# A four-layer diffusion backbone: gate products of a GLA head moved between its own levels, low-rank gates in two passes, and products moved ahead of the first attention scores

## The chip, the cores and the metric

The kernel runs on one NeuronCore of a Trainium2 chip. TensorE (PE) multiplies matrices, VectorE (DVE), ScalarE (ACT) and GpSimd (POOL) do elementwise work, and SyncE (SP) and ACT issue most of the DMAs. The metric is the device time of one execution in microseconds; a kernel's time is the median of its runs.

## The reference

A latent stream of 512 tokens and a context stream of 256 tokens, each 1024 wide, run through four layers. Layer i uses mixer i % 3: layers 0 and 3 are a bidirectional chunked GLA (gated linear attention, 4 heads), layer 1 is a windowed attention with a sink, layer 2 a bidirectional RG-LRU. Layer 3 gives no context output (`ctx_out` is false there).

```python
def mixer_gla(h_lat, h_ctx, w_in, w_g1, w_g2, b_g, g_head, w_out, ctx_out):
    def project(h):
        q, k, v, z = jnp.split(h @ w_in, [GLA_DK, 2 * GLA_DK, 2 * GLA_DK + GLA_DV], axis=-1)
        la_f, la_b = [split_heads(jax.nn.log_sigmoid(((h @ w_g1[d]) @ w_g2[d] + b_g[d]).astype(jnp.float32)) / GLA_TAU, GLA_HEADS)
                      for d in range(2)]
        ...
    def finish(o, z):
        o = merge_heads(rmsnorm(o, g_head[:, None, :]))
        return (o.astype(z.dtype) * jax.nn.silu(z)) @ w_out
...
    for i in range(DEPTH):
        ...
        h = rmsnorm(x, g_pre[i]) * (1.0 + scale[:, None, :]) + shift[:, None, :]
        ...
        x = x + gate[:, None, :] * rmsnorm(y, g_post[i])
```

Here `w_g1` is the low-rank gate (rank 16, two directions), and z is the gate product: each head's output is multiplied by silu(z) before the product with `w_out`.

## The kernel before

All activations lie transposed in SBUF: a tile holds 128 features on its partitions and the 768 tokens along its free axis (512 latent, "lat", then 256 context, "ctx"). A product with full precision is made of three matmul passes: every operand is split into a rounded part and a remainder (`Rh`, `Rl` for activations, `wh`, `wl` for weights), and Rh·wh, Rl·wh and Rh·wl are summed in PSUM. A 128-column block of weights over both streams is 8 contraction steps × 3 passes × two widths: 24 matmuls of 256 columns and 24 of 512.

**Stages.** `first_norm` (0 to 62 us) normalises the input, makes the modulation of layer 0 (L524) and begins the first products (L728), among them the g1 product. Then come GLA layer 0 (62 to 370 us), `finish` of layer 0 (products with w_out, L796), attention, its finish, RG-LRU, its finish, GLA layer 3 (about 1207 to 1460 us) and its finish.

**Weights.** `plan(i)` yields a layer's weight blocks in the order in which they are multiplied. `loadw` issues the DMAs of a block (two pieces of 512 KB, on SP's queue), and `convert` splits it: an ACT copy to `wh` (L266) and a DVE subtraction to `wl` (L269). `weights(key)` hands out the next block, and keeps up to two ahead. `load_g1` (L271 on) loads the 32 columns of the low-rank gate, and splits them four times over into four 32-column groups of a `wh` and a `wl` tile (L287), so that the product `t` = g1·h comes out four times on 128 partitions. The gate product (L979) uses 96 of these, against a three-group tile `g2`.

**A GLA head.** For each head h: `gates(h)` makes its decays, `project(h)` its q and k (L385), and `levels` walks over the levels of a chunk from the smallest up (L1062 score matmuls of 24 pieces, with X, Y and K made by DVE, ACT and POOL before them). Between the levels, `spread` deals out matmuls of a side stream: a generator that yields each matmul with its cost in columns. The side stream is z(h-1), then v(h) (L1034): the gate product of the head before and the head's own values. Head 0 has no head before, and so v(0) alone. `outputs(h)` comes in the next head: transposes (L1155), state updates (L1166), output products (L1194), the head's norm, and transposes back (L1207). The gate product z of a head (`z_steps`, its matmuls at L395) ends in silu, and is multiplied with the head's output in `OG`: whichever of the two comes first writes `OG`, and the other multiplies (`put` keeps account). Head 3's outputs come after the loop, and then z(3): `run(outputs(*prev))`, `run(zgates(GH - 1))`. A scheduler then sets the final order by priorities, and may pull those z products up between the output's steps.

**Attention.** `fill(n)` puts n columns' worth of waiting product matmuls (L395) into the program; the loop over the heads' blocks calls it after the scores of each block (L1458 to L1475), then transposes the probabilities (L1516) and multiplies them with v (L1532).

## Time and profile before

| | us |
|---|---|
| median of 3 runs | 1517.19 (1516.3 to 1522.14) |
| the profiled execution | 1513.64 |
| its span in the trace | 1511.8 |
| PE busy | 1442.0 (95%) |
| DVE busy | 1010.5 (67%) |
| ACT busy | 784.2 (52%) |
| GLA layer 0, 62 to 370.05 | 308.1 |
| GLA layer 3, 1207 to 1460.82 | 253.8 |

The trace is that of one execution, whose own time is 1513.64 us, 3.55 us under the median; 1.8 us of it lie outside the span. A matmul's row gives its whole duration; one starts before the last one's end, so what a stream of matmuls costs is the distance between starts. A value in square brackets behind a row is the idle time ahead of it, with what ended it. "Clock" is TensorE's granted clock as a share of 2.4 GHz.

### The profile page before, as it was taken

What the parts mean: (1) busy time and instruction counts of PE and PEld (TensorE: products, weight loads), DVE (VectorE), ACT (ScalarE), POOL (GpSimd) and SP (SyncE); (2) the same over time, 40 slices, a digit from 0 to 9 for tenths busy, and PEclk for the clock granted to TensorE, in tenths of its full rate; (3) what the DMA queues carried; (4) which work ended last, traced back from release to release, by engine and by line L of the source; (5) the groups of instructions that cost most, each with busy time, mean ns of one, the idle gap of its engine ahead of it and who ended that gap; (6) DMA issues with size and microseconds to landing.
All of it is one profiled execution on the core that took longest, in us unless ns stands there. A gap on an engine that the chain in (4) does not pass through costs nothing.

```text
span 1511.8 us, 29077 instructions
## 1 busy us (share of the span) xinstructions
PE 1442.0 (95%) x11691; PEld 1206.4 (80%) x11691; DVE 1010.5 (67%) x1914; ACT 784.2 (52%) x1541; POOL 189.4 (13%) x300
## 2 busy tenths in 40 slices
PE   5988999999999899999999999899999999999998
PEld 3877888888877778878888787788878778889886
DVE  5576657576264389787883568988972667676854
ACT  5535353624252367656662477878842555364441
POOL 2202100112022200010000210000011211101111
PEclk8999999999999999999999999999999999999999
DMA  9441514112574542122216625212252342121232
GB/s 300 145 147 53 169 38 135 57 34 76 203 237 140 174 112 68 31 65 57 57 56 224 217 79 152 82 50 71 67 177 64 103 145 91 46 60 57 60 111 85
DMA packets 153046, 162.35 MB, mean 107 GB/s; under 512 B 12418, under 2 KB 141968, under 8 KB 152912
## 3 DMA queue, kind: packets, MB, share of 16 engines
q1 hardware_dynamic: 147456, 146.56, 31.4%
q10 hardware_dynamic: 5456, 13.94, 2.6%
q8 instruction: 92, 1.51, 0.4%
q14 instruction: 42, 0.34, 0.1%
HBM read 138.44 MB, written 11.53 MB: 99 GB/s over the span
## 4 chain that ended last, share of the span: by engine, by line
PE 54%; DVE 10%; ACT 5%; DMA 4%; issue 2%; SPq 1%; POOL 1%; ACTq 0%; DVEq 0%; POOLq 0%
PE mxt L796 14%; PE pjt L395 9%; PE pjt L385 9%; PE pjt L1034 4%; PE mxt L1532 3%; PE mxt L1516 2%; PE sct L1637 2%; PE mxt L524 1%; PE mxt L1475 1%; PE mxt L1194 1%; DVE wl L269 1%; PE mxt L1458 1%; DMA bb<-in_b_mod_dram 1%; DMA raw<-in_w_mod_dram 1%; PE sct L1062 1%
## 5 line engine op out<-in xcount | busy, mean ns | idle before, releaser
L385 PE MATMUL pjt<-Rh,wh 128*128 128x256 f32 (+1 forms) x592 | 199.0, 337 | 5.3 <-DVE Rh L649 3.3
L385 PE MATMUL pjt<-Rl,wh 128*128 128x256 f32 (+1 forms) x592 | 198.2, 336 | 2.0 <-DVE Rl L650 1.6
L385 PE MATMUL pjt<-Rh,wl 128*128 128x256 f32 (+1 forms) x592 | 197.1, 334 | 0.7 <-DVE wl L269 0.7
L269 DVE TENSOR_TENSOR wl<-raw,wh 128x1024 fp32r<-128x1024 f32 x106 | 129.7, 1237 | 51.2 <-ACT wh L266 50.6
L395 PE MATMUL pjt<-Rh,wl 128*128 128x512 f32 (+1 forms) x448 | 160.3, 358 | 0.0
L395 PE MATMUL pjt<-Rl,wh 128*128 128x512 f32 (+1 forms) x448 | 159.8, 357 | 0.0
L395 PE MATMUL pjt<-Rh,wh 128*128 128x512 f32 (+1 forms) x448 | 159.5, 356 | 0.0
L266 ACT CAST wh<-raw 128x1024 fp32r<-128x1024 f32 x118 | 121.4, 1051 | 71.6 <-PE mxt L796 33.0
L796 PE MATMUL mxt<-wh,Rh 128*128 128x512 f32 x352 | 138.9, 395 | 0.0
L796 PE MATMUL mxt<-wh,Rl 128*128 128x512 f32 x352 | 137.6, 391 | 0.8 <-DVE Rl L769 0.8
L796 PE MATMUL mxt<-wl,Rh 128*128 128x512 f32 x352 | 137.2, 390 | 0.0
L385 PEld LDWEIGHTS pjt<-Rh,wh 128*128 128x128 f32 x592 | 112.5, 191 | 17.0 <-DVE Rh L649 4.4
L385 PEld LDWEIGHTS pjt<-Rl,wh 128*128 128x128 f32 x592 | 112.6, 190 | 14.6 <-DVE Rl L650 3.8
L385 PEld LDWEIGHTS pjt<-Rh,wl 128*128 128x128 f32 x592 | 112.6, 191 | 12.6 <-DVE wl L269 1.2
L1034 PE MATMUL pjt<-wl,Rh 128*128 128x256 f32 x384 | 110.6, 288 | 0.0
L1034 PE MATMUL pjt<-wh,Rh 128*128 128x256 f32 x384 | 109.8, 286 | 0.0
L1034 PE MATMUL pjt<-wh,Rl 128*128 128x256 f32 x384 | 109.5, 285 | 0.0
L1494 ACT ACTIVATE pe<-mxt,mxs 128x256 f32<-128x256 f32 (+2 forms) x128 | 70.7, 556 | 52.6 <-DVE mxs L1486 51.9
L395 PEld LDWEIGHTS pjt<-Rh,wl 128*128 128x128 f32 x448 | 84.6, 189 | 9.8 <-issue 1.9
L395 PEld LDWEIGHTS pjt<-Rh,wh 128*128 128x128 f32 x448 | 84.7, 189 | 9.2 <-issue 1.2
L395 PEld LDWEIGHTS pjt<-Rl,wh 128*128 128x128 f32 x448 | 84.7, 189 | 9.2 <-issue 1.3
L804 DVE TENSOR_TENSOR y<-mxt,gpt 128x512 f32<-128x512 f32 x44 | 30.3, 689 | 73.9 <-ACT y L803 73.8
(295 smaller groups left out, 3480.9 us busy)
## 6 DMA issues: line engine op xcount, KB each, us to landing
rawp<-in_w_mod_dram SPq DMA_DIRECT2D x48, 512.0 KB, 5.8
raw<-in_w_mod_dram SPq DMA_DIRECT2D x48, 512.0 KB, 4.4
raw<-in_a_w_in_dram SPq DMA_DIRECT2D x32, 512.0 KB, 3.5
raw<-in_b_w_in_dram SPq DMA_DIRECT2D x20, 512.0 KB, 4.9
raw<-in_c_w_in_dram SPq DMA_DIRECT2D x20, 512.0 KB, 3.6
xd<-x SPq DMA_DIRECT2D x18, 512.0 KB
raw<-in_a_w_out_dram SPq DMA_DIRECT2D x16, 512.0 KB, 3.5
x<-xd ACTq DMA_DIRECT2D x16, 512.0 KB, 8.9
```

The source lines that it names most:

```text
L266: S.copy(h, x)
L269: e.tensor_tensor(l, x, h.bitcast(F32), op=ALU.subtract)
L385: PE.matmul(ps, w[u][:, k, c0 : c0 + P], R[v][:, k, t0 : t0 + n], start=(k == 0 and u + v == 0), stop=(k == KC - 1 and u == 1),)
L395: PE.matmul(ps, w[u][:, k, c0 : c0 + P], R[x][:, k, t0 : t0 + n], start=(k == 0 and u + x == 0), stop=(k == KC - 1 and u == 1),)
L524: PE.matmul(ps[32 * g : 32 * g + 32, 0:256], sT[:, k, :], r2[k // 4][:, k % 4, :], start=(n < 4), stop=(n >= 4), skip_group_check=True,)
L796: PE.matmul(ps, l[:, tt * P : (tt + 1) * P], r, start=(k == 0 and u + v == 0), stop=(k == kc - 1 and u == 1),)
L804: V.tensor_tensor(y[tt][:, c], ps, gpt[:, 1 if tt >= 4 else 0, c], op=ALU.mult)
L1034: PE.matmul(ps[:, n, :], R[u][:, k, tt * P : (tt + 1) * P], w[x][:, k, :], start=(k == 0 and u + x == 0), stop=(k == KC - 1 and u == 1),)
L1494: S.activation(p[:, o : o + w], u[e][:, :w], AF.Exp, bias=nm, scale=0.125, accum_out=den[:, n : n + 1],)
L1516: PE.transpose(u[e][:, c * P : (c + 1) * P], ps[e][:, m * P : (m + 1) * P], ident)
L1532: PE.matmul(po[64 * e : 64 * e + 64, 0:P], v[:, keys[m], 64 * kv : 64 * kv + 64], pt[:, e, m * P : (m + 1) * P], start=(m == len(keys) - 1 ...
L1637: PE.matmul(ps[:, t0 : t0 + nn], wg[a][:, n, :], x[c][:, p0 : p0 + nn], start=(q == 0), stop=(q == 2),)
```

## The change

Three things are changed.

- **g1 in two passes.** `load_g1` makes one tile with four 32-column groups: the rounded weights three times and their remainder once (one ACT copy from the raw tile, one DVE subtraction, two more ACT copies). `terms(w)` then gives two passes, w·Rh and w·Rl, in place of three: the low-order weight product comes out on partitions of its own. `g2` gets a fourth row group (one more DMA of 32 KB on each of the ACT and SP queues), and the gate matmul contracts over 128 partitions instead of 96.
- **z with its own head.** In `plan` and in the loop over heads, heads 0 to 2 have z(h) and then v(h) as side stream. In head 3 the side stream is v(3), then the first half of z(3) (e = 0); the second half (e = 1) comes after the outputs.
- **Attention.** `fill(2300)` is called once more, ahead of the first block's scores.

```diff
--- before.py
+++ after.py
@@ -270,6 +270,7 @@
 
     def load_g1(a):
 
         r = raw()
         rv = r.rearrange("p a b -> p (a b)")[:, 0:256].rearrange("p (k r) -> p k r", k=KC)
         for d in range(2):
@@ -279,13 +280,12 @@
             )
 
         def convert():
-            w1h = wp.tile([P, KC, 256], F32R, name="wh", tag="wh")
-            w1l = wp.tile([P, KC, 256], F32R, name="wl", tag="wl")
-            for g in range(4):
-                c = slice(32 * g, 32 * g + 32)
-                S.copy(w1h[:, :, c], rv)
-                V.tensor_tensor(w1l[:, :, c], rv, w1h[:, :, c].bitcast(F32), op=ALU.subtract)
-            return w1h, w1l
+            w1 = wp.tile([P, KC, 256], F32R, name="wh", tag="wh")
+            S.copy(w1[:, :, 0:32], rv)
+            V.tensor_tensor(w1[:, :, 96:128], rv, w1[:, :, 0:32].bitcast(F32), op=ALU.subtract)
+            for g in range(1, 3):
+                S.copy(w1[:, :, 32 * g : 32 * g + 32], w1[:, :, 0:32].bitcast(F32))
+            return (w1,)
 
         return convert
 
@@ -299,7 +299,7 @@
         if load:
             g2_loaded.append(a)
             for d in range(2):
-                for g in range(3):
+                for g in range(4):
                     (nc.sync if d else nc.scalar).dma_start(
                         r[32 * g + 16 * d : 32 * g + 16 * d + 16, d, :], I["a_w_g2"][a, d]
                     )
@@ -324,10 +324,9 @@
             qk = lambda h: (f"qk{h}", cols(w, (h * P, P), (512 + h * P, P)))
             v = lambda h: (f"v{h}", cols(w, (1024 + h * GDV, GDV)))
             z = lambda h: (f"z{h}", cols(w, (2048 + h * GDV, GDV)))
-            yield from (qk(0), v(0))
-            for h in range(1, GH):
-                yield from (qk(h), z(h - 1), v(h))
-            yield z(GH - 1)
+            for h in range(GH - 1):
+                yield from (qk(h), z(h), v(h))
+            yield from (qk(GH - 1), v(GH - 1), z(GH - 1))
         elif kind == 1:
             w, wo = I["b_w_in"][0], I["b_w_out"][0]
             q = lambda g: (f"q{g}", cols(w, (g * 256, 256)))
@@ -377,14 +376,18 @@
 
     begun = {}
 
+    def terms(w):
+        return ((0, 0), (0, 1), (1, 0)) if len(w) > 1 else ((0, 0), (0, 1))
     def ws_part(w, c0, ps, t0, n):
 
         R = (Rh, Rl)
         for k in range(KC):
-            for u, v in ((0, 0), (0, 1), (1, 0)):
+            for u, v in terms(w):
                 PE.matmul(
                     ps, w[u][:, k, c0 : c0 + P], R[v][:, k, t0 : t0 + n],
-                    start=(k == 0 and u + v == 0), stop=(k == KC - 1 and u == 1),
+                    start=(k == 0 and u + v == 0), stop=(k == KC - 1 and (u, v) == terms(w)[-1]),
                 )
 
     def product_steps(ps, w, c0, t0, n):
@@ -724,11 +727,11 @@
             for w, c0, stream, ps in sel:
                 t0, n = STREAM[stream]
                 for k in ks:
-                    for u, v in ((0, 0), (0, 1), (1, 0)):
+                    for u, v in terms(w):
                         PE.matmul(
                             ps, w[u][:, k, c0 : c0 + P], (Rh, Rl)[v][:, k, t0 : t0 + n],
                             start=(k == 0 and u + v == 0 and not (w is wqk and stream == "ctx")),
-                            stop=(k == KC - 1 and u == 1), skip_group_check=True,
+                            stop=(k == KC - 1 and (u, v) == terms(w)[-1]), skip_group_check=True,
                         )
 
         with tc.manual_schedule(engines={PE.engine, S.engine, V.engine}):
@@ -943,6 +946,7 @@
             keep_pool.append(1)
             g2r = load_g2(a)
             w1 = weights("g1")
             t1 = mp.tile([P, T], F32R, name="t1")
             for stream in ("ctx", "lat"):
                 t0, n = STREAM[stream]
@@ -953,7 +957,7 @@
                 )
 
             g2 = mp.tile([P, 2, 512], F32R, name="g2")
-            S.copy(g2[:96], g2r[:96])
+            S.copy(g2, g2r)
             G.tensor_tensor(g2[32:64], g2r[32:64], g2[32:64].bitcast(F32), op=ALU.subtract)
 
             gated = {}
@@ -977,7 +981,7 @@
                     for stream in ("ctx", "lat"):
                         t0, n = STREAM[stream]
                         PE.matmul(
-                            ps[:, t0 : t0 + n], g2[:96, d, h * P : (h + 1) * P], t1[:96, t0 : t0 + n],
+                            ps[:, t0 : t0 + n], g2[:, d, h * P : (h + 1) * P], t1[:, t0 : t0 + n],
                             start=True, stop=True,
                         )
                     S.activation(tmp[:, pl, :], ps[:, :T], AF.Abs, bias=b)
@@ -1250,9 +1254,13 @@
                     background(1)
                     yield
 
-            def zgates(h):
-                w = weights(f"z{h}")
-                for e in range(2):
+            wz = {}
+            def zgates(h, es=(0, 1)):
+                if h not in wz:
+                    wz[h] = weights(f"z{h}")
+                w = wz[h]
+                for e in es:
                     for stream in ("ctx", "lat") if ctx_out else ("lat",):
                         yield from z_steps(mp, w, e, 2 * h + e, put, (stream,))
 
@@ -1275,7 +1283,6 @@
                 Y = mp.tile([P, 2, T], F32, name="Y", tag="Y", bufs=2)
                 pr = project(h, q, Y)
                 os = outputs(*prev) if prev else iter(())
-                z = zgates(h - 1) if prev else iter(())
                 next(pr)
                 next(os, None)
                 next(pr)
@@ -1302,15 +1309,19 @@
                     vl.rearrange("p d t -> p (d t)").rearrange("p (c n) -> p c n", c=6),
                 )
 
-                side = chain(z, values(h, v))
                 nz = len(STREAM) * T if ctx_out else len(STREAM) * TL
-                nz = nz if prev else 0
-                spread(lv, side, len(LEVELS), 24 * (nz + 4 * GDV) / 2.4)
+                if h < GH - 1:
+                    side = chain(zgates(h), values(h, v))
+                    spread(lv, side, len(LEVELS), 24 * (nz + 4 * GDV) / 2.4)
+                else:
+                    side = chain(values(h, v), zgates(h, (0,)))
+                    spread(lv, side, len(LEVELS), 24 * (nz // 2 + 6 * GDV) / 2.4)
                 run(side)
                 run(mods(2))
                 prev = (h, X, Y, A, v, tl)
             run(outputs(*prev))
-            run(zgates(GH - 1))
+            run(zgates(GH - 1, (1,)))
             keep_pool.clear()
         finish_args[0] = (KC, None)
 
@@ -1548,6 +1559,8 @@
                 while b not in todo:
                     fill(100)
                     credit = 0
+                if not b:
+                    fill(2300)
                 for qt in (4, 0, 1, 5, 3, 2):
                     new = scores(b, qt)
                     done, turned = turned, (turn(*scored) if scored else None)
```

In head 0 of GLA layer 0, PE's order at the first of the level scores that need K (`L1062 sct<-X,K`, called L1066 in the changed kernel) was this; `pjt<-wh,Rh` and the like are matmuls of v(0), L524 and L582 belong to the modulation of the next layer:

```order
L1034 MATMUL pjt<-wl,Rh 128x256
L1034 MATMUL pjt<-wh,Rl 128x256
L1062 MATMUL sct<-X,K 32x32 x24
L1034 MATMUL pjt<-wh,Rh 128x256
L524 MATMUL mxt<-raw,sT 32x256 x8
L582 MATMUL mxt<-mh,sel 128x256
L582 MATMUL mxt<-ml,sel 128x256
L582 MATMUL mxt<-mh,sel 128x256
L582 MATMUL mxt<-ml,sel 128x256
L1062 MATMUL sct<-X,K 32x32 x24
```

In the changed kernel the four blocks of K scores stand each between 18 or 19 product matmuls; the last of them:

```order
L1038 MATMUL pjt<-wl,Rh 128x256
L1038 MATMUL pjt<-wh,Rl 128x256
L1038 MATMUL pjt<-wh,Rh 128x256
L1066 MATMUL sct<-X,K 32x32 x24
L1038 MATMUL pjt<-wl,Rh 128x256
L1038 MATMUL pjt<-wh,Rl 128x256
```

The z(0) matmuls (48 of 256 columns and 48 of 512) now stand ahead of these, between the first levels, and 73 matmuls of v(0) are left behind the last level.

At the end of GLA layer 0 PE had a run of z(3) matmuls, ending so:

```order
L395 MATMUL pjt<-Rh,wh 128x512
L395 MATMUL pjt<-Rl,wh 128x512
L395 MATMUL pjt<-Rh,wl 128x512
L796 MATMUL mxt<-wh,Rh 128x512
L796 MATMUL mxt<-wl,Rh 128x512
```

Now the finish (L799) follows the head's last transposes (L1211) at once, with 48 z(3) matmuls in all between the steps of the outputs, the last seven between the two transposes:

```order
L398 MATMUL pjt<-Rh,wl 128x512
L398 MATMUL pjt<-Rh,wh 128x512
L1211 MATMUL mxt<-ident,on 128x128 x4
L545 MATMUL mxt<-ident,mp 128x128 x2
L799 MATMUL mxt<-wh,Rh 128x512
L799 MATMUL mxt<-wl,Rh 128x512
```

At the end of GLA layer 3, PE's last output products (L1194), transposes and 25 z(3) matmuls were mixed, the last 11 of these between L582 and L796. Now no product stands behind the outputs' first steps (the L1198 are the output products):

```order
L1198 MATMUL mxt<-v,Al 128x256
L1198 MATMUL mxt<-st,X 128x256 x2
L1211 MATMUL mxt<-ident,on 128x128 x8
L585 MATMUL mxt<-mh,sel 128x256
L585 MATMUL mxt<-ml,sel 128x256
L585 MATMUL mxt<-mh,sel 128x256
L585 MATMUL mxt<-ml,sel 128x256
L799 MATMUL mxt<-wh,Rh 128x512
```

In attention, PE's order ahead of the first scores is the same in both (24 products of 256 columns and 24 of 512, then L1475). Products are taken earlier after that, and at the end of the stage the transposes of the last block (L1516) had eight products behind them, in two groups:

```order
L1516 MATMUL mxt<-ident,pe 128x128 x8
L395 MATMUL pjt<-Rl,wh 128x512
L395 MATMUL pjt<-Rh,wl 128x512
L395 MATMUL pjt<-Rh,wh 128x512
L1516 MATMUL mxt<-ident,pe 128x128 x2
```

Now none is left there:

```order
L398 MATMUL pjt<-Rh,wl 128x512
L1527 MATMUL mxt<-ident,pe 128x128 x10
L1543 MATMUL mxt<-pt,v 64x128 x10
L585 MATMUL mxt<-mh,sel 128x256
L585 MATMUL mxt<-ml,sel 128x256
```

## Rows read from the trace of the kernel before

**Rows 1.** The page's head: span, and busy time of each engine.

```profile
span 1511.8 us, 29077 instructions
...
PE 1442.0 (95%) x11691; PEld 1206.4 (80%) x11691; DVE 1010.5 (67%) x1914; ACT 784.2 (52%) x1541; POOL 189.4 (13%) x300
```

**Rows 2.** Busy time by stretch; head row names the columns; stretches begin at L1166.

```profile
core 0: us, PE busy (x) PEld busy (x) DVE busy (x) ACT busy (x) POOL busy (x), PEclk, DMA share, GB/s
...
62.00:114.98 52.98, 48.12 (x712) 41.12 (x711) 37.84 (x58) 25.42 (x39) 4.96 (x7) 0.97 0.48 147
114.98:199.94 84.96, 79.17 (x909) 67.29 (x908) 52.54 (x82) 35.45 (x64) 13.79 (x23) 1.00 0.35 111
199.94:276.27 76.33, 75.22 (x871) 65.24 (x870) 49.34 (x80) 33.70 (x60) 8.42 (x16) 1.00 0.29 86
...
1207.00:1267.31 60.31, 58.25 (x636) 49.69 (x634) 41.74 (x63) 29.85 (x45) 10.81 (x14) 0.97 0.43 133
1267.31:1328.29 60.98, 60.08 (x604) 51.93 (x602) 41.08 (x64) 29.02 (x49) 5.90 (x14) 1.00 0.20 60
1328.29:1387.57 59.28, 59.28 (x604) 51.66 (x602) 40.93 (x64) 29.30 (x49) 6.31 (x14) 1.00 0.19 58
```

**Rows 3.** PE's timeline, g1 matmuls in first_norm: start us, us, what.

```profile
56.85 0.28 PE L728 MATMUL sct<-Rh,wh 128*128 128x256 f32 x1
56.97 0.28 PE L728 MATMUL sct<-Rl,wh 128*128 128x256 f32 x1
```

**Rows 4.** PE's timeline in head 0 of layer 0, at the first K scores.

```profile
90.80 1.11 PE L1062 MATMUL sct<-X,K 128*32 128x32 f32 x48 [3.44 <-ACT K L1096]
...
92.36 1.94 PE L524 MATMUL mxt<-raw,sT 128*32 128x256 f32 x16
```

**Rows 5.** ACT's waits from 62 to 115 us: us in total, times, longest.

```profile
ACT wh L266 <- DMA raw<-in_a_w_in_dram: 7.0, 3, 4.0
ACT K L1096 <- DVE Y L1110: 5.3, 2, 4.2
```

**Rows 6.** Busy time by stretch (columns as in rows 2) behind two PE waits.

```profile
90.80:94.30 3.50, 3.50 (x66) 1.89 (x66) 2.79 (x3) 1.33 (x3) 0.00 (x0) 0.51 0.08 23
...
528.60:532.00 3.40, 3.40 (x28) 3.31 (x29) 1.04 (x2) 0.00 (x0) 0.00 (x0) 1.00 0.59 135
```

**Rows 7.** PE's timeline in the outputs of head 0.

```profile
117.86 0.44 PE L1155 MATMUL mxt<-ident,Y 128*128 128x128 f32 x2 [1.21 <-DVE ktl L1159]
...
120.16 0.39 PE L1166 MATMUL mxt<-v,kth 128*128 128x256 f32 x1 [1.63 <-ACT st L1177]
```

**Rows 8.** PE's timeline: the rest of z(3) after layer 0's outputs.

```profile
361.75 0.37 PE L395 MATMUL pjt<-Rl,wh 128*128 128x256 f32 x1
...
370.05 0.39 PE L796 MATMUL mxt<-wh,Rh 128*128 128x512 f32 x1
```

**Rows 9.** The chain that ended last, at g1's split ahead of layer 3.

```profile
1188.76 1.43 DVE wl L287 x4
```

**Rows 10.** PE's timeline, g1 of layer 3 (latent half).

```profile
1208.30 0.41 PE L385 MATMUL pjt<-Rl,wh 128*128 128x256 f32 x1
1208.51 0.41 PE L385 MATMUL pjt<-Rh,wl 128*128 128x256 f32 x1
```

**Rows 11.** PE's timeline at the end of layer 3's outputs.

```profile
1453.69 0.63 PE L1207 MATMUL mxt<-ident,on 128*128 128x128 f32 x4
...
1456.45 0.60 PE L1207 MATMUL mxt<-ident,on 128*128 128x128 f32 x4
...
1460.82 0.39 PE L796 MATMUL mxt<-wh,Rh 128*128 128x512 f32 x1
```

**Rows 12.** PE's timeline in attention: first scores, last transposes and heads.

```profile
528.60 0.38 PE L1475 MATMUL mxt<-khi,q 128*128 128x256 f32 x1 [2.35 <-DVE q L1389]
...
787.08 0.48 PE L395 MATMUL pjt<-Rl,wh 128*128 128x512 f32 x1
...
789.32 1.31 PE L1532 MATMUL mxt<-pt,v 128*64 128x128 f32 x20
```

## The prediction

> **What bounds the kernel now.** I read the page's head first: PE is busy for 1442.0 of 1511.8 us [rows 1], so only two things can move the time much: matmuls that vanish, and the 70 us in which PE stands. The next view is busy time by stretch, cut at the first state update (L1166) of each head of the GLA layers, so that neighbouring rows hold the same work [rows 2]. In layer 0, PE stands 52.98 - 48.12 = 4.86 us in head 0, 84.96 - 79.17 = 5.79 us in the period behind it, and only 76.33 - 75.22 = 1.11 us in the next one. In layer 3 the same three stretches have 2.06, 0.90 and 0 us. So it is the first head of each layer that loses time, the head whose side stream was short. Third, the waits there: the K scores of head 0 came 3.44 us late [rows 4], behind an ACT copy that waited for DVE (4.2 us at the longest), and ACT had before that waited 4.0 us for a piece of `a_w_in` in one go [rows 5]. ACT and DVE were not full (25.4 and 37.8 of 53.0 us, rows 2); they were late. After that wait the granted clock was 0.51 for 3.5 us [rows 6], that is, the lower of the two levels, and 16 modulation matmuls took 1.94 us [rows 4].
>
> Moving z does not remove a matmul: what head 0 takes on (two blocks of 24 matmuls of 256 columns and 24 of 512) head 3 and the tail give up. The tail's rest of z(3), 23 of 256 and 24 of 512 columns, ran from 361.75 to 370.05 us, 8.30 us [rows 8]; with 0.12 us for 256 columns [rows 3] that leaves 0.231 us for one of 512, and a whole z is about 16.8 us. The gain is only what PE no longer waits, and so I count waits, part by part.
>
> **The change part by part.** All terms are made against the profiled execution of 1513.64 us (span 1511.8 us), which lies 3.55 us under the median of 1517.19; the sum is then carried to the median.
>
> 1. *g1 in first_norm.* Eight contraction steps lose one pass at 0.12 + 0.231 = 0.35 us each: 2.8 us in all. The first four steps stand ahead of modulation matmuls that wait for their weights' DMA, and save nothing there; the last four lie in a dense run [rows 3]. So -1.4 us (0 to -2.8). The three low-order copies that DVE no longer makes are hidden there. The two more small DMAs, one on ACT's and one on SP's queue, are an issue each, ahead of a tile that is needed at the first gate product; I price them at nothing, and at most at the 1.4 us that this term saves, if they delay the raw pieces queued behind them.
> 2. *Head 0 of layer 0.* Lost before: 4.86 us of standing and 3.5 x 0.49 = 1.7 us to the lower clock [rows 2, 6], 6.6 us. The order shows why less is lost now: after the first levels, every K block had one filler or 46 in front of it, now 18 or 19, which are 2.2 us, near what the later heads have. Against it, ACT and DVE must now split z(0)'s weights and make its silu too, with two more table loads on ACT. ACT has 27 us free in the stretch and 16 more us come; I leave half of the loss: -3.3 us (+2 to -6.6).
> 3. *The period behind it (outputs of head 0).* It stands 5.79 - 1.11 = 4.7 us more than the period after it [rows 2], with the waits for `ktl` and `st` of 1.21 and 1.63 us [rows 7]. These are remains of head 0's lateness: the next periods have the same outputs and no such waits. In the changed kernel, 73 matmuls of v(0) and the q and k products of head 1 stand behind the last level, in which ACT and DVE catch up. -4.4 us (0 to -4.7).
> 4. *The end of layer 0.* z(3)'s rest goes, its work having been counted in head 0, but it also covered the head's norm. In layer 3 that chain, from one group of transposes to the next, took at most 1456.45 - 1453.69 = 2.76 us [rows 11]. Seven matmuls of 512 columns, 1.6 us, are left over it here, and 1.1 us could show; +0.8 us (0 to 2.8). What comes next is L799, whose first products need only the early blocks of OG.
> 5. *Start of layer 3.* DVE's four subtractions lie on the chain that ended last, 1.43 us for four [rows 9]; three go: -1.07 us. The latent half of g1 loses 8 matmuls of 256 columns: 0.12 us each [rows 3], or 0.21 at the lower clock that they had [rows 10]: -0.96 us. Together -2.0 us (0, if the DMA behind the split sets the end instead, to -2.8).
> 6. *Heads 0 and 1 of layer 3.* 2.06 us of standing, and a period of 60.98 against 59.28 us [rows 2], 3.8 us to be had, some of it ahead of head 0's levels; -2.4 us (0 to -3.8).
> 7. *End of layer 3.* Here no product at all is left over the norm's chain of 2.76 us, of which the PE's own transposes are part; 11 products which stood ahead of L796 do not cover anything of their own. +1.9 us (0.5 to 3.5).
> 8. *Attention.* The wait of 2.35 us before the first scores [rows 12] stays, since no product more stands ahead of it in the order; this part does not do what its place suggests. The products are taken sooner, so that between the last transposes and the last heads (787.08 to 789.32 us, 2.24 us [rows 12]) there is none. I take +1.0 us, nearer to that row than to nothing, since the blocks in the middle may gain from fuller gaps (-2 to +3.5).
>
> Sum: -1.4 - 3.3 - 4.4 + 0.8 - 2.0 - 2.4 + 1.9 + 1.0 = **-9.8 us**: 1503.8 us for an execution like the profiled one, 1507.4 us on the median.
>
> **The rivals.** *Nothing gained in the heads.* ACT and DVE are as late as before, since head 0 lost its time to a weights' DMA [rows 5] and z(0)'s pieces come ahead of v(0)'s on the same queue. Then terms 2, 3 and 6 are zero: -1.4 + 0.8 - 2.0 + 1.9 + 1.0 = +0.3, 1517.5 us. For it speaks the DMA wait; against it, that PE has 16.8 us more to do while the pieces come.
>
> *The tails drop the clock.* If PE stands for some 3 us at the end of attention and of layer 3, the finish behind it starts at the lower level. A wait of 3.44 us was followed by 3.5 us at 0.51, one of 2.35 us by full clock [rows 4, 6, 12]; 1.7 us for each. With both tails at their upper ends: -9.8 + 2 x 1.7 + 1.6 + 2.5 = -2.3, 1514.9 us. The Trainium skill's page TensorE: Matmul & The Clock Gate, section "HAM oscillation — how this bites in real kernels", says that a TensorE that idles between bursts of matmuls falls back to half rate, so that the next burst starts slow. This speaks against the attention and layer 3 parts of the change; the trace agrees for the longer of the two waits and not for the shorter.
>
> *Slower: the splits of v(0) block ACT.* z(0)'s two pieces and its two splits are put ahead of v(0)'s, and behind a split that waits for its DMA stand, on ACT in order, the K copies, the silu of z(0), and so the PSUM banks that PE needs. Each such wait costs what the one of before cost: 3.44 us and 1.7 us of clock, 5.1 us. Two in each layer's head 0 give -9.8 + 20.4 = +10.6, 1527.8 us. It decides from about three and a half such waits on, where the sum passes +7.6 us. For it: ACT waited three times for DMA in that stretch, 7.0 us. Against it: the DMA engines were busy 0.48 of it, and in the next periods, with z and v both loaded, 0.35 and 0.29 [rows 2], and PE hardly stood.
>
> **How the numbers follow.** The forecast has 0.68, nothing gained in the heads 0.14, the tails 0.13, the slower one 0.05. About 0.5% of the median (7.6 us) is what a measurement of this kernel can tell from no change, so faster means below 1509.6 us. Of the forecast, 0.10 lies above that, if head 0 keeps more of its loss than half: faster 0.58, within 0.5% 0.37, slower 0.05. The range of 1501 to 1516 us reaches from -16 us (terms 3, 5 and 6 at full size, head 0 at -5, the tails of layers 0 and 3 at their lower ends) up past the tails' rival, and leaves out most of the first rival and the slower one.
>
> **What would show it.** The trace after should have the first L1170 of layer 0 some 12 us later than 115 us (16.8 of z less about 4.7), its next period near 80 us, no wait of over 1.5 us in head 0, and full clock around 91 us. The finish of layer 0 should begin near 361.8 us, and layer 3 should take about 2.5 us less, with some 2 us of standing in front of its L799. The first scores should still wait over 2 us. Wrong would be: a wait for ACT's splits in head 0, the stands of the second period back in place, or a clock of 0.51 behind either tail.

## The result, and the profile after

The changed kernel takes 1528.09 us (median of 13 runs, 1522.79 to 1532.04), the kernel before 1519.78 us (13 runs, 1513.9 to 1525.03): a ratio of 1.0061 with a 95% interval of 1.0048 to 1.0074. It is slower by 8 to 9 us, where 9.8 us less were forecast. With more runs the median of before rose from 1517.19 to 1519.78 us, so that the profiled execution that the prediction read is one of the quickest; the trace after is of an execution of 1528.86 us. Differences between single traces are therefore read here only where several kernels repeat them. One execution of att_reserve was slow (1596.15 us at a granted clock of 0.845); it counts in the median below and not in the ratio.

The page's head of the changed kernel answers to [rows 1]:

```profile
span 1525.7 us, 28973 instructions
...
PE 1442.8 (95%) x11651; PEld 1205.1 (79%) x11651; DVE 1014.7 (67%) x1908; ACT 779.7 (51%) x1524; POOL 186.5 (12%) x302
```

32 matmuls went with g1 (the trace counts 40 fewer), and PE's busy time is the same: what went as work came back as matmuls at the lower clock, and what the span grew by is PE standing (69.8 us before, 82.9 us now). Busy time by stretch of the changed kernel (us, then busy time and count of PE, PEld, DVE, ACT, POOL, granted clock, DMA share, GB/s): head 0 of layer 0, the two periods that answer to [rows 2], then the end of attention, layer 3's last head and its outputs.

```profile
62.00:130.35 68.35, 64.29 (x811) 55.06 (x809) 44.80 (x66) 32.53 (x48) 8.68 (x13) 1.00 0.45 139
130.35:210.81 80.46, 78.29 (x909) 66.92 (x908) 49.78 (x79) 33.13 (x59) 9.42 (x17) 1.00 0.36 109
210.81:287.43 76.62, 75.19 (x871) 65.23 (x870) 48.91 (x79) 32.58 (x57) 8.44 (x16) 1.00 0.27 85
...
781.04:796.08 15.04, 11.08 (x78) 8.82 (x78) 13.84 (x32) 11.03 (x26) 1.32 (x2) 0.89 0.24 75
...
1403.93:1453.38 49.45, 48.97 (x545) 43.02 (x544) 36.88 (x60) 26.07 (x45) 2.35 (x4) 1.00 0.14 47
1453.38:1474.13 20.75, 16.38 (x88) 13.76 (x86) 16.76 (x33) 9.35 (x26) 6.95 (x14) 0.87 0.16 51
```

The same three last stretches of the kernel before:

```profile
779.46:791.14 11.68, 11.68 (x93) 9.66 (x92) 10.74 (x26) 9.93 (x27) 0.00 (x0) 1.00 0.14 46
...
1387.57:1440.20 52.63, 52.63 (x562) 45.71 (x561) 38.78 (x63) 27.84 (x48) 6.31 (x14) 1.00 0.15 44
1440.20:1460.82 20.62, 20.58 (x119) 17.29 (x118) 14.36 (x29) 9.94 (x26) 1.77 (x4) 1.00 0.17 52
```

Layer 0 did what was forecast: the second period stands 2.2 us where it stood 5.8. What PE waited for in head 0 and this period (62 to 210.81 us) in the changed kernel, in us in total, times and longest:

```profile
PE mxt L527 <- DMA raw<-in_w_mod_dram: 4.4, 4, 1.8
PE sct L1066 <- ACT K L1100: 1.0, 1, 1.0
PE mxt L585 <- ACT mh L578: 0.4, 1, 0.4
PE sct L1066 <- DVE X L1114: 0.3, 1, 0.3
```

The waits for `ktl` and `st` [rows 7] are gone, and the K scores wait 1.0 us. ACT, too, waits less for its weights: 3.5 to 4.7 us for pieces of `a_w_in` in this stretch in the seven kernels with the z move in layer 0, and 9.2 to 10.6 us from 62 to 200 us in the five without it.

The two ends did not do what was forecast. At the end of attention 15 matmuls have gone, 3.4 us of work, and the stretch is 3.4 us longer; in layer 3's last outputs 31 have gone (119 to 88), 7.1 us of work at 0.23 us each, and the stretch is as long as ever. PE's timeline shows both ends (start, us, what, in brackets the idle time ahead and what ended it):

```profile
790.63 0.76 PE L1527 MATMUL mxt<-ident,pe 128*128 128x128 f32 x5 [2.37 <-DVE pe L1514]
792.78 2.35 PE L1543 MATMUL mxt<-pt,v 128*64 128x128 f32 x20 [1.39 <-ACT pt L1532]
795.06 0.58 PE L585 MATMUL mxt<-mh,sel 128*128 128x256 f32 x1
...
1461.49 0.39 PE L1170 MATMUL mxt<-v,kth 128*128 128x256 f32 x1 [1.91 <-DVE ktl L1163]
1463.56 0.41 PE L1170 MATMUL mxt<-vl,kth 128*128 128x256 f32 x1
1463.77 0.41 PE L1170 MATMUL mxt<-v,ktl 128*128 128x256 f32 x1
...
1472.12 1.08 PE L1211 MATMUL mxt<-ident,on 128*128 128x128 f32 x4 [1.82 <-DVE on L1204]
1474.13 0.79 PE L799 MATMUL mxt<-wh,Rh 128*128 128x512 f32 x1
```

PE stands in each, and behind each stand its matmuls are slow: 20 of L1543 take 2.35 us where they took 1.31 [rows 12], and the state updates stand 0.21 us apart, not 0.12. That is the lower of the two clock levels.

### The profile page after: what moved, and what is told of

It is laid out like the page before. It is cut to its first block, busy times and chain, and to the rows that moved or that the text cites. A ratio compares the mean times of both kernels' runs of the same rounds, so it can differ in the third digit from the quotient of the medians.

```text
span 1525.7 us, 28973 instructions
## 1 busy us (share of the span) xinstructions
PE 1442.8 (95%) x11651; PEld 1205.1 (79%) x11651; DVE 1014.7 (67%) x1908; ACT 779.7 (51%) x1524; POOL 186.5 (12%) x302
## 4 chain that ended last, share of the span: by engine, by line
PE 65%; DVE 14%; DMA 9%; ACT 7%; issue 3%; SPq 1%; POOL 1%; ACTq 0%; DVEq 0%; POOLq 0%
PE mxt L799 15%; PE pjt L388 12%; PE pjt L398 9%; PE pjt L1038 7%; DMA raw<-in_w_mod_dram 3%; PE mxt L1198 3%; PE mxt L527 3%; PE mxt L1543 3%; PE mxt L1527 2%; PE sct L1650 2%; DVE wl L269 2%; PE mxt L1170 2%; PE sct L1066 1%; PE mxt L1486 1%; PE mxt L1469 1%
## 5 line engine op out<-in xcount | busy, mean ns | idle before, releaser
L388 PE MATMUL pjt<-Rh,wl 128*128 128x256 f32 (+1 forms) x568 | 189.9, 335 | 0.8 <-DVE wl L269 0.8
L269 DVE TENSOR_TENSOR wl<-raw,wh 128x1024 fp32r<-128x1024 f32 x106 | 130.1, 1241 | 59.9 <-ACT wh L266 59.5
L398 PE MATMUL pjt<-Rh,wh 128*128 128x512 f32 (+1 forms) x448 | 158.6, 354 | 0.0
L799 PE MATMUL mxt<-wh,Rh 128*128 128x512 f32 x352 | 139.5, 397 | 0.1
L799 PE MATMUL mxt<-wh,Rl 128*128 128x512 f32 x352 | 137.8, 392 | 0.8 <-DVE Rl L772 0.8
L799 PE MATMUL mxt<-wl,Rh 128*128 128x512 f32 x352 | 137.5, 391 | 0.0
L388 PEld LDWEIGHTS pjt<-Rh,wl 128*128 128x128 f32 x568 | 107.8, 190 | 12.6 <-DVE wl L269 1.2
L398 PEld LDWEIGHTS pjt<-Rh,wl 128*128 128x128 f32 x448 | 84.7, 189 | 9.5 <-issue 1.6
```

The costliest lines, as they stand in the source:

```text
L269: e.tensor_tensor(l, x, h.bitcast(F32), op=ALU.subtract)
L388: PE.matmul(ps, w[u][:, k, c0 : c0 + P], R[v][:, k, t0 : t0 + n], start=(k == 0 and u + v == 0), stop=(k == KC - 1 and (u, v) == terms(w)[ ...
L398: PE.matmul(ps, w[u][:, k, c0 : c0 + P], R[x][:, k, t0 : t0 + n], start=(k == 0 and u + x == 0), stop=(k == KC - 1 and u == 1),)
L799: PE.matmul(ps, l[:, tt * P : (tt + 1) * P], r, start=(k == 0 and u + v == 0), stop=(k == kc - 1 and u == 1),)
```

## The experiments

Ten more kernels were run, each a part or a variant of the change. Theory A, formed from the two traces: the change gains in layer 0 what was forecast, and loses where products no longer cover a chain of DVE and ACT steps, at the end of attention and of layer 3. Theory B: the new waits come from weights' DMAs and shifted timing, and any part of the change could show them. Each table row gives the median and the ratio to the kernel before from runs on the same chip; not all rows are from one chip, so that between rows the ratios are compared, and not the medians.

| kernel | median us (runs) | before us (runs) | ratio, 95% interval |
|---|---|---|---|
| the change | 1528.09 (13) | 1519.78 (13) | 1.0061, 1.0048 to 1.0074 |
| g1_alone | 1517.96 (12) | 1518.75 (32) | 0.9994, 0.9980 to 1.0009 |
| z_alone | 1518.53 (12) | 1518.75 (32) | 0.9997, 0.9983 to 1.0011 |
| fill_alone | 1527.01 (9) | 1518.75 (32) | 1.0061, 1.0041 to 1.0082 |
| g1_z_no_fill | 1520.90 (12) | 1518.75 (32) | 1.0020, 1.0006 to 1.0033 |
| g1_z_layer0 | 1507.35 (6) | 1517.43 (19) | 0.9935, 0.9923 to 0.9948 |
| z3_after | 1512.31 (8) | 1517.43 (19) | 0.9973, 0.9959 to 0.9988 |
| att_reserve | 1517.04 (12) | 1517.43 (19) | 1.0000, 0.9984 to 1.0015 |
| dummy_tail | 1523.25 (6) | 1517.43 (19) | 1.0040, 1.0025 to 1.0055 |
| z_layer0 | 1509.46 (9) | 1516.10 (15) | 0.9953, 0.9936 to 0.9970 |
| layer0_padded | 1508.88 (7) | 1516.10 (15) | 0.9954, 0.9935 to 0.9973 |

And this is one trace of each, cut into stretches by PE's timeline (us). "Layer 0" ends with the first product of finish 0; "to scores" is finish 0 and the projections of attention; "scores" runs from the first scores to the last block's; "end" from there to the first product of finish 1; "fin 2, head 0" is from the start of finish 2 to the first state update of layer 3; "heads 1, 2" the next two periods; "head 3" from there to the start of finish 3.

| kernel | layer 0 | to scores | scores | end | fin 2, head 0 | heads 1, 2 | head 3 |
|---|---|---|---|---|---|---|---|
| before | 370.0 | 158.6 | 250.9 | 11.7 | 162.5 | 120.3 | 73.2 |
| g1_alone | 371.8 | 160.1 | 253.2 | 11.7 | 159.8 | 120.2 | 73.2 |
| fill_alone | 372.9 | 162.4 | 256.7 | 15.1 | 161.0 | 120.2 | 73.3 |
| att_reserve | 372.8 | 158.4 | 252.2 | 11.6 | 161.3 | 120.3 | 73.2 |
| dummy_tail | 371.7 | 159.1 | 256.8 | 11.8 | 161.4 | 120.3 | 73.3 |
| z_alone | 362.9 | 159.4 | 251.6 | 11.7 | 174.4 | 119.6 | 70.2 |
| g1_z_no_fill | 363.2 | 160.7 | 253.5 | 11.7 | 173.5 | 119.7 | 70.0 |
| the change | 363.2 | 159.9 | 258.0 | 15.0 | 173.4 | 119.9 | 70.2 |
| z3_after | 362.8 | 160.1 | 252.9 | 11.7 | 172.6 | 119.6 | 64.3 |
| g1_z_layer0 | 361.4 | 161.0 | 251.7 | 11.7 | 160.0 | 120.2 | 73.3 |
| z_layer0 | 365.1 | 158.4 | 252.4 | 11.7 | 161.3 | 120.3 | 73.2 |
| layer0_padded | 360.8 | 160.4 | 253.5 | 11.7 | 161.5 | 120.2 | 73.3 |

### The three parts, each alone

**g1_alone** has only the two passes of g1, with g2's fourth group:

```diff
-            return w1h, w1l
+            return (w1,)
...
-                for g in range(3):
+                for g in range(4):
```

> The kernel before with only the two-pass g1 product (and g2's fourth row group). Theory A (covers that ran out: the change loses in attention and at the end of layer 3, where product matmuls no longer cover a chain): 2.5 us faster than before (1 to 3.5), 1.4 us in first_norm and the rest ahead of layer 3. Theory B (the new waits come from weights' DMAs and from when ACT and DVE are free, which any shift in time can move): within 1 us of before.

Measured: 0.9994, no change that can be told. Theory A's 2.5 us would be 0.9984, which lies just inside the interval; so does theory B's 1 us, so that this run does not decide between them.

**z_alone** has only the z products moved:

```diff
-            for h in range(1, GH):
-                yield from (qk(h), z(h - 1), v(h))
-            yield z(GH - 1)
+            for h in range(GH - 1):
+                yield from (qk(h), z(h), v(h))
+            yield from (qk(GH - 1), v(GH - 1), z(GH - 1))
...
+                    side = chain(values(h, v), zgates(h, (0,)))
...
-            run(zgates(GH - 1))
+            run(zgates(GH - 1, (1,)))
```

> The kernel before with only the z products moved to their own heads. Theory A: layer 0 gains 5.5 us, layer 3 loses 7 us, at its last head and its end above all, where 4 to 5 us are PE standing and a clock of 0.5 behind it; in sum 1.5 us slower (2 faster to 4 slower). Theory B: both layers vary with the DMA of weights, layer 3's end within 2 us of before, in sum 4 to 8 us faster.

Measured: 0.9997. It is no change because two larger ones cancel: layer 0 takes 362.9 us against 370.0 to 372.9 in the five kernels without the move, and from finish 2 to finish 3 layer 3 takes 364.2 (174.4 + 119.6 + 70.2) against 353 to 356. Theory A had the sum right, within its range, and both halves too small; theory B's 4 to 8 us faster did not come.

**fill_alone** has only this:

```diff
+                if not b:
+                    fill(2300)
```

> The kernel before with only the extra fill(2300) ahead of the first scores. Theory A: 8 to 11 us slower, all of it in attention: some 4 us of standing at its end with the clock at 0.5 behind, the rest ahead of that. Theory B: within 3 us of before; attention's loss in the changed kernel came from the later start and the weights' DMAs there.

Measured: 1.0061, the ratio of the whole change. Theory A's 8 to 11 us came, and theory B's 3 us did not. Its waits at the end of attention are those of the changed kernel. What engine waited for which line, PE from 791 to 808 us (us in total, times, longest):

```profile
PE mxt L1527 <- DVE pe L1514: 2.6, 2, 2.4
PE mxt L1543 <- ACT pt L1532: 1.4, 1, 1.4
```

**g1_z_no_fill** is the changed kernel with those two lines taken out again.

> The changed kernel without the extra fill(2300). Theory A: attention as long as before (421 us from the start of finish 0 to that of finish 1 within 3 us), and 0 to 3 us faster than before in all. Theory B: still 5 to 9 us slower than before.

Measured: 1.0020. This is 3 us slower than before, not 0 to 3 faster, and far from theory B's 5 to 9. Attention from finish 0 to finish 1 takes 425.8 us in its trace: 4.7 more than in the trace of before, and so outside theory A's 3 us, but the other kernels without the fill take 421 to 426 us, and the two with it and an uncovered end 433 and 434. The fill's share inside the change, by the two ratios (1.0061 and 1.0020), is some 6 us. The 0.2% more than z_alone stays within what two intervals leave open.

### Attention: the end or the middle

**att_reserve** keeps the extra fill and takes as much from the last two blocks' fills, so that products are left for the end:

```diff
-                    credit = fill(credit + 2300)
+                    credit = fill(credit + (2108 if b > 5 else 2300))
```

> The kernel before with the extra fill(2300) ahead of the first scores, and 192 columns' time less in each of the last 12 fills, so that the products for the end of attention are as many as before. Theory A (the loss of 9 us is that the end stood, and the clock behind it): 1 to 4 us slower than before, the end of attention (last scores to the first L796-type matmul) within 1 us of the 11.7 us before. Theory B (the fills in the middle are what costs): 7 to 10 us slower.

Measured: 1.0000 (0.9984 to 1.0015). The end is back at 11.6 us without a wait, the stretch of the scores at 252.2 us. Theory B's 7 to 10 us are out; theory A had the end right, and of its 1 to 4 us of loss the interval leaves 2.3 at most. So within some 2 us products taken ahead of the first scores neither cost nor gain, as long as the end keeps as many.

**dummy_tail** keeps the whole extra fill and puts 11 matmuls which nobody reads at the end:

```diff
                     yield from z_block(kv)
+                yield from cover()
...
+            def cover():
+                ps = pjt()[:, :TL]
+                for k in range(11):
+                    PE.matmul(ps, last[0][0][:, k % 8, 0:P], Rh[:, k % 8, 0:TL], start=(k == 0), stop=(k == 10))
+                    yield TL / 2.4
```

> The kernel before with the extra fill(2300), and 11 matmuls of 512 columns into an unread bank as last products, which the scheduler puts between the last transposes and the last heads, where products stood before; they add 2.5 us of work that the reference doesn't need. Theory A: with the end covered, PE doesn't stand there and the clock stays full, so that 2.5 us of added work make the kernel 4 to 5 us faster than with the extra fill alone, and 4 to 5 us slower than before. Theory B: 2 to 3 us slower than with the extra fill alone, 11 to 12 us slower than before.

Measured: 1.0040 (1.0025 to 1.0055), 6 us slower than before. That is less than theory B's 11 to 12, and more than theory A's 4 to 5 though its interval takes these in. By the medians it is 3 us less than fill_alone's 1.0061 with 2.5 us of work more, but the two intervals overlap, and so the end itself is read from the traces. Here is the end of attention by busy time, first in fill_alone, with the first 4 us of finish 1, then the same two in dummy_tail:

```profile
791.98:807.07 15.09, 11.13 (x78) 8.87 (x78) 13.84 (x32) 11.03 (x26) 1.32 (x2) 0.85 0.25 73
807.07:811.00 3.93, 3.93 (x14) 3.15 (x14) 1.45 (x3) 0.00 (x0) 0.00 (x0) 0.71 0.89 304
```

```profile
787.68:799.48 11.80, 11.80 (x90) 9.45 (x89) 8.71 (x24) 8.04 (x21) 0.71 (x2) 1.00 0.16 46
799.48:803.48 4.00, 4.00 (x19) 2.99 (x18) 4.00 (x7) 2.61 (x6) 0.00 (x0) 1.00 0.87 299
```

With 12 matmuls more the end is 3.3 us shorter: PE does not stand, the clock stays full, and finish 1 begins at full clock (19 matmuls in its first 4 us, not 14). The stretch of the scores is 256.7 and 256.8 us in the two, and 250.9 to 253.5 us without the fill (and in att_reserve), 4 to 5 us less on average. So the 15 products (3.4 us) that were moved into it did not fill waits there; they lengthened it, and PE stands 8.1 to 9.5 us in it in the three kernels with the whole fill, 5.5 to 6.9 us in the others. That is most of the 6 us which dummy_tail still loses.

### Layer 3: what its last outputs need

**g1_z_layer0** leaves layer 3's z products as they were, without the fill:

```diff
-            for h in range(GH - 1):
-                yield from (qk(h), z(h), v(h))
-            yield from (qk(GH - 1), v(GH - 1), z(GH - 1))
+            if i == 0:
+                for h in range(GH - 1):
+                    yield from (qk(h), z(h), v(h))
+                yield from (qk(GH - 1), v(GH - 1), z(GH - 1))
+            else:
+                yield from (qk(0), v(0))
+                for h in range(1, GH):
+                    yield from (qk(h), z(h - 1), v(h))
+                yield z(GH - 1)
```

> The changed kernel without the extra fill, and with the z products of layer 3 dealt out as before; so what is left is g1 in two passes and the z products of layer 0. Theory A (layer 0 gains 8.5 us as its stretch up to the first L796 showed with and without the change, 363 against 371.6 us; layer 3 loses 9 us as its heads have too little to cover the last outputs): 8 us faster than before (6 to 10). Theory B (what layer 0 gains is given back where the next stages wait for weights): within 3 us of before.

Measured: 0.9935 (0.9923 to 0.9948), 10 us faster than before, as theory A had it. It has the lowest ratio of all, though the intervals of z_layer0 and layer0_padded below overlap its own.

**z3_after** is the changed kernel without the fill; it keeps z(0) to z(2) with their own heads and puts all of z(3) after the outputs, in both layers:

```diff
-                    side = chain(values(h, v), zgates(h, (0,)))
-                    spread(lv, side, len(LEVELS), 24 * (nz // 2 + 6 * GDV) / 2.4)
+                    side = values(h, v)
+                    spread(lv, side, len(LEVELS), 24 * 4 * GDV / 2.4)
...
-            run(zgates(GH - 1, (1,)))
+            run(zgates(GH - 1))
```

> The changed kernel without the extra fill, and with all of z(3) after the outputs of head 3 (in both GLA layers), so that head 3's levels have only v(3). Theory A (the last outputs of layer 3 are bound by their own chain, and need the 41 matmuls that they had before): the last outputs are covered again, no clock of 0.5 there; layer 3 loses 3 us instead of 9, and the kernel is 3 us faster than before (1 to 5). Theory B (head 3's levels then wait as head 0's did): layer 3 as slow as with the change, 0 to 3 us slower than before.

Measured: 0.9973 (0.9959 to 0.9988), some 4 us faster than before, within theory A's 1 to 5. Layer 3's last head with the same matmuls as in z_alone takes 64.3 us, not 70.2. Busy time in z_alone (levels, then outputs), then in z3_after:

```profile
1394.62:1444.38 49.76, 48.95 (x546) 43.02 (x545) 36.90 (x60) 26.04 (x45) 2.35 (x4) 1.00 0.15 47
1444.38:1464.79 20.41, 15.71 (x87) 13.04 (x86) 16.73 (x33) 9.32 (x26) 6.94 (x14) 0.92 0.16 51
```

```profile
1394.68:1437.37 42.69, 42.02 (x514) 37.57 (x513) 33.57 (x56) 22.83 (x40) 2.31 (x4) 1.00 0.10 30
1437.37:1458.98 21.61, 20.93 (x118) 17.20 (x118) 15.92 (x31) 10.71 (x28) 7.45 (x14) 1.00 0.16 49
```

The outputs take 20.4 us with 87 matmuls and 21.6 us with 118. So they are bound by their own chain, and 31 products more, 7.1 us of work, fit into it for 1.2 us (a little more at equal clock: the shorter one had a granted clock of 0.92). The levels without z(3) stand no more than with it (0.67 against 0.81 us), so theory B's rival wait is not there.

### What g1 is worth

**z_layer0** is g1_z_layer0 with g1 in three passes again; **layer0_padded** is g1_z_layer0 with eight matmuls put ahead of the first g1 products in first_norm:

```diff
+                    for _ in range(4 if k == 0 and len(w) == 1 else 0):
+                        PE.matmul(
+                            ps, w[0][:, k, c0 : c0 + P], Rh[:, k, t0 : t0 + n],
+                            start=True, stop=False, skip_group_check=True,
+                        )
```

> The kernel before with only layer 0's z products moved to their own heads (g1 in three passes as before, no extra fill, layer 3 as before). Theory A (g1's shorter work saves 1.6 us ahead of layer 3 and nothing in first_norm): 8 us faster than before, 1 to 2 us slower than with g1 in two passes. Theory B (g1 saves nothing): 10 us faster, like the kernel with g1 in two passes.

> g1 in two passes and layer 0's z products moved, as in g1_z_layer0, and in first_norm four extra matmuls of 256 columns and four of 512 ahead of the first two g1 products, whose sums the first real pass overwrites: 1.4 us of work that the reference doesn't need, in the place of the passes that g1 lost ahead of the modulation's weights. Theory A (PE waits for those weights anyway): as g1_z_layer0 within its interval, no clock of 0.5 between 40 and 47 us, and the wait for the weights at about 42 us 1 to 1.5 us shorter than the 2.1 and 3.0 us of the changed kernel and of g1 alone. Theory B (PE is the bound there): 1.4 us slower than g1_z_layer0.

Measured: 0.9953 and 0.9954, against 0.9935 with g1 in two passes; the intervals overlap, and what g1 is worth in the end can't be told from these runs, nor which theory holds. The traces say where it can be found. PE's timeline in first_norm at the wait for the modulation's weights, the g1 products behind it, and the first gate product (L984, L994), in g1_alone and then in layer0_padded:

```profile
41.56 1.07 PE L528 MATMUL pjt<-rawp,sT 128*32 128x256 f32 x16 [3.02 <-DMA rawp<-in_w_mod_dram]
...
43.40 0.42 PE L732 MATMUL sct<-Rh,wl 128*128 128x256 f32 x1
43.62 0.41 PE L732 MATMUL sct<-Rh,wh 128*128 128x256 f32 x1
43.83 0.41 PE L732 MATMUL sct<-Rl,wh 128*128 128x256 f32 x1
...
65.38 0.87 PE L984 MATMUL sct<-t,g 128*128 128x256 f32 x4
```

```profile
41.29 1.07 PE L533 MATMUL pjt<-rawp,sT 128*32 128x256 f32 x16 [1.35 <-DMA rawp<-in_w_mod_dram]
...
42.75 0.28 PE L742 MATMUL sct<-Rh,wh 128*128 128x256 f32 x1
42.87 0.28 PE L742 MATMUL sct<-Rl,wh 128*128 128x256 f32 x1
42.99 0.28 PE L742 MATMUL sct<-Rh,wl 128*128 128x256 f32 x1
...
63.51 0.87 PE L994 MATMUL sct<-t,g 128*128 128x256 f32 x4
```

The modulation product at this place (L528, L533) starts at 41.1 to 41.9 us in all twelve traces, whatever stands ahead of it, so passes saved ahead of it only lengthen PE's wait. From there to the first gate product the twelve fall into three groups:

| g1 | clock behind the wait | us from the modulation product to the gate product | kernels |
|---|---|---|---|
| three passes | full | 23.62 to 23.64 | before, fill_alone, att_reserve, dummy_tail, z_alone, z_layer0 |
| two passes | full | 22.21 to 22.22 | g1_z_layer0, z3_after, layer0_padded |
| two passes | lower level for 3.4 us | 23.79 to 23.82 | the change, g1_alone, g1_z_no_fill |

So the last four steps of g1 do save 1.4 us, and a drop of the clock, with matmuls of 256 columns 0.21 us apart in place of 0.12, takes 1.6 us and with it all of the gain. The padding, ahead of the wait, costs nothing there, as theory A had it. The waits in the third group were 2.10, 3.02 and 1.91 us, those in the second 2.59, 3.08 and 1.35, and dummy_tail's was 2.15: the length of the wait alone does not decide whether the clock drops, and what else does was not tried.

## Why the prediction was wrong

The forecast was -9.8 us, the time 1528.09 us, outside its range. The likeliest case failed in two terms, 7 and 8, which priced the chains that the moved products had covered far too low, and by less in a third, term 6; the terms of layer 0 held in sum.

- **Terms 1 to 4, layer 0: right in sum.** -8.3 us was forecast; the kernels of the table without the move give 370.0 to 372.9 us, those with it 360.8 to 365.1, some 9 us. The first state update was to come at about 127 us and came at 130.35 (128.2 to 130.1 in the other kernels with the move in layer 0), the period behind it was to take about 80 us and took 80.46, finish 0 was to begin at 361.8 us and began at 363.19. The K scores wait 1.0 us at the most in head 0, where they waited 2.8 to 3.9 us without the move, and the clock is full there, as terms 2 and 3 had it. Term 2's reason is right only in part: in the trace the four blocks of K scores had 46, 1, 14 and 8 products ahead of them, not one or 46, and the wait of 3.44 us came behind the 46; the changed kernel has 17 to 19 ahead of each. What goes with the shorter wait in every kernel is that ACT waits less for `a_w_in`; no run took that apart from the fillers. One wait of 1.65 us in that head, for a piece of the next modulation's weights, is over the 1.5 us that were named as a limit. Term 1's -1.4 us in first_norm did not show in the changed kernel: its size was right where the clock stayed full, and here a drop of the clock behind the wait for the modulation's weights took it back, which the term did not have.
- **Term 5, start of layer 3: right in sign, and half the size.** -2.0 us forecast; among the kernels with layer 3's z products as before, "fin 2, head 0" takes 159.8, 160.0 and 161.5 us with g1 in two passes, 161.0 to 162.5 without: -1.1 us on average. The two groups just overlap; among the kernels with layer 3's z products moved it is 172.6 to 173.5 against z_alone's 174.4, about as much.
- **Term 6, heads 0 and 1 of layer 3: wrong in sign.** -2.4 us forecast. Head 0 has 48 matmuls more, 10.9 us, and its stretch grew by 12.8 us (z_alone against the four kernels up to dummy_tail that have g1 in three passes and no move, 161.6 on average), heads 1 and 2 shrank by 0.7: about +1 us. Head 0 of this layer had little standing to fill: of the 2.06 us of [rows 2], 0.61 and 0.57 us were waits for pieces of the next modulation's weights, which come with or without z, and 0.76 us was a wait of the K scores, which came down to 0.57 us.
- **Term 7, the end of layer 3: mis-sized, +1.9 us forecast, +7.8 us measured.** Without z(2)'s 10.9 us, head 3 should have taken 62.4 us, and took 70.2. The working asked what the chain of the last norm would show, 2.76 us [rows 11]. It did not ask what the 31 products which left the steps before had covered. In that stretch PE had been full with 119 matmuls, and this was read as PE being the bound; the chain behind it was as long: with 31 matmuls fewer it took 20.75 us, as before. PE stood 4.4 us in it, and the granted clock was 0.87.
- **Term 8, attention: mis-sized, +1.0 us forecast, +9 us measured.** The order did show that no product was left between the last transposes and the last heads. The term then credited the middle with a gain from products that come sooner. fill_alone and dummy_tail show none: the moved products lengthened the middle by what they take, or more. At the end, where nothing covers it, they left 4 us of standing, and then the lower clock for some 3.4 us in the changed kernel and 6.8 us in fill_alone. The +9 us is fill_alone's; inside the change g1_z_no_fill puts the fill at some 6 us. That the first scores would still wait over 2 us was wrong too: they waited 0.25 us in the changed kernel, 2.9 in fill_alone and 0.3 in g1_alone, so that this wait goes by timing and not by the fill.
- **The rivals.** The second rival, the tails that drop the clock, is the one that happened: the clock was at the lower level behind the stands of both ends, though in attention it fell on the last heads, and the first 4 us of finish 1 in the changed kernel had no more than a trace of it (18 matmuls, 0.97). Its price of 1514.9 us was too low by 13 us, since it took over term 6 and had the ends of terms 7 and 8 at 3.5 us each. The page TensorE: Matmul & The Clock Gate of the Trainium skill, section "HAM oscillation — how this bites in real kernels", which was weighed there, says that a TensorE which idles between bursts starts the next at half rate; these traces agree at both ends, behind waits of 1.4 to 2.4 us, and do not in first_norm, where waits of 2.59 and 3.08 us were followed by the full clock. The slower rival, ACT blocked by splits of v(0), did not come: ACT has no wait for `a_w_in` in head 0 of layer 0, from 62 to 130 us, and PE stood 4.1 us in 62 to 130 us. The change is slower for another reason, so that this rival's time, 1527.8 us, is near the measured one by accident.

By the parts as measured, layer 0 gives -9, the start of layer 3 -1.1, its heads +1.2, its end +7.8, attention +9: +8 us, against 8.3 to 9.3 us. That the sum fits so well is in part luck: without attention the same parts give -1 us, and g1_z_no_fill is 3 us slower than before (1 to 5 by its interval). So 2 to 6 us of that kernel have no place in this account; whether the fill costs less in the change than alone, the intervals leave open.

## What to carry to other kernels

A product that is moved earlier is a cover taken from where it stood: ask of that place how long its chain is without it, step by step, not only at the last step, and whether PE was full there because it was the bound or because somebody had put enough work over a chain of the same length. A PE-bound stretch that gets shorter work gains only down to that chain, here 20.4 us with 87 matmuls and 21.6 us with 118. A move that helps in one layer need not in its twin with narrower products: layer 0 gained 9 us, layer 3 lost as much, and doing it in layer 0 alone gives 10 us.

## What the runs showed that was not expected

- Work taken from ahead of a DMA wait gains nothing there, and the clock may fall behind the longer wait: g1 in two passes saved 1.4 us behind it in three kernels, and in three others a drop took 1.6 us and left nothing of that.
- The clock is not decided by the length of one wait alone: waits of 2.10 and 1.91 us in first_norm were followed by the lower clock, waits of 2.59 and 3.08 us in the same place were not.
- 11 matmuls that nobody reads, 2.5 us of work, made the end of attention 3.3 us shorter (11.80 us, against 15.09 in fill_alone).
